# A prefix log-sum-exp scan: constants off the path to the first load, the last Exp behind the Ln of the tile above, and one late load split by partition groups

## The chip, the cores and the metric

The kernel runs on one core of a Trainium2 chip. The metric is the device time of one execution in microseconds (us), lower is better. The kernel before takes 1258.24 us (median of 4 runs, 1258.01 to 1258.38). "The trace" is one profiled execution; times in it count from the start of its span, which is about 1.8 us shorter than the device time. "Landing" means the moment at which the last of the 16 DMA engines has raised a DMA's semaphore; the trace records each of these increments.

## The reference

For each of 8 batches and 2048 columns, a running log-sum-exp over 4096 positions:

```python
out[:, 0, :] = x[:, 0, :]
for t in range(1, S):                       # S = 4096
    mx = np.maximum(out[:, t-1, :], x[:, t, :])
    out[:, t, :] = mx + np.log(np.exp(out[:, t-1, :] - mx) + np.exp(x[:, t, :] - mx))
```

Input and output are float32, 268.44 MB each.

## The kernel before

The work is cut into 64 tiles of 512 positions by 2048 columns: 128 partitions, 4 rows each, 4 MB (32 KB per partition). ScalarE (ACT) takes Exp of a quarter of a tile (512 columns), TensorE multiplies by triangular matrices of ones to get prefix sums, VectorE (DVE) adds up the 4 rows of a partition in place, ACT takes Ln, and the tile is stored. Five tile buffers go round: a load waits until the store from its buffer has landed.

```python
Li = const.tile([P, P], bf16)
masks.make_upper_triangular(nc, Li, val=1.0, diag=True)      # and Ls, Ui, Us, on POOL,
...                                                          # ahead of the block below
@block.sync
def _(sp):                                                   # the load queue
    def load(src, n):
        sp.dma_start(out=io[n][:], in_=src).then_inc(loaded[n], 16)
    for i in range(NB):                                      # NB = 5 buffers
        load(x_v[i], i)
    ...                                                      # loop over tiles 5 to 59
    for i in range(NB + turns * NB, NT):                     # tiles 60 to 63, NT = 64
        take(sp, stored[i % NB], 16)                         # wait for the store, then subtract
        load(x_v[i], i % NB)
...
@block.scalar
def _(act):                                                  # ACT, and the store queue
    def turn(n, dst_above):
        exp(n, 0)                                            # waits for loaded[n]
        if dst_above is not None:
            ln(io[(n - 1) % NB], 2)                          # last two quarters of the tile above
        exp(n, 1)
        if dst_above is not None:
            ln(io[(n - 1) % NB], 3)
            store(dst_above, (n - 1) % NB)                   # waits for 4 Ln, issues 4 MB
        exp(n, 2)
        ln(io[n], 0)
        exp(n, 3)
        ln(io[n], 1)
    ...
    # after tile 63: store its first half, then Ln and store of its last two quarters
```

The softmax here doesn't subtract the row's maximum and nothing guards it: scores larger than these inputs give would overflow.

Of the kernel before, what the change touches and what calls it, by code (L numbers as in the profile page):

```python
# [9 lines left out]
def kernel(  # L10
# [20 lines left out]
    nc = tc.nc  # L31
# [5 lines left out]
    B, S, D = x.shape  # L37
    P = 128
    R = 4
    NBLK = S // (P * R)  # L40
    NT = B * NBLK
    FD = 512
    NC = D // FD
    NB = 5
    assert NC == 4 and NBLK >= 3

    const = ctx.enter_context(tc.tile_pool(name="const", bufs=1))
    Li = const.tile([P, P], bf16)
    masks.make_upper_triangular(nc, Li, val=1.0, diag=True)
    Ls = const.tile([P, P], bf16)  # L50
    masks.make_upper_triangular(nc, Ls, val=1.0, diag=False)
    Ui = const.tile([P, P], bf16)
    masks.make_lower_triangular(nc, Ui, val=1.0, diag=True)
    Us = const.tile([P, P], bf16)
    masks.make_lower_triangular(nc, Us, val=1.0, diag=False)

    pool = ctx.enter_context(tc.tile_pool(name="io", bufs=1))
    psum = ctx.enter_context(tc.tile_pool(name="ps", bufs=1, space=bass.MemoryType.PSUM))
# [26 lines left out]
    with tc.tile_critical():  # L85
# [10 lines left out]
        chain = [sem("chain0"), sem("chain1")]  # L96
        freed = [sem("freed0"), sem("freed1")]

        with nc.Block() as block:

            @block.sync
            def _(sp):
                def load(src, n):
                    sp.dma_start(out=io[n][:], in_=src).then_inc(loaded[n], 16)

                for i in range(NB):
                    load(x_v[i], i)
                turns = (NT - NB) // NB
                with sp.Fori(0, turns) as j:
                    for n in range(NB):  # L110
                        take(sp, stored[n], 16)
                        load(x_v[bass.ds(j * NB + (NB + n), 1)][0], n)
                for i in range(NB + turns * NB, NT):
                    take(sp, stored[i % NB], 16)
                    load(x_v[i], i % NB)
                for i in range(NT - NB, NT):

                    take(sp, stored[i % NB], 48 if i == NT - 1 else 16)

            @block.scalar  # L120
            def _(act):
                def exp(n, c):
                    t = io[n]
                    if c == 0:
                        take(act, loaded[n], 16)
                    act.activation(  # L126
                        et[c][:], t[:, :, cols(c)], ACT.Exp
                    )._wait_ge(freed[c % 2], c // 2 + 1).then_inc(exps[c % 2], 1)
                    if c >= 2:
                        take(act, freed[c % 2], 2)  # L130

                def ln(t, c, told=logs):
                    act.activation(  # L133
                        t[:, :, cols(c)], t[:, :, cols(c)], ACT.Ln
                    )._wait_ge(added[c % 2], c // 2 + 1).then_inc(told, 1)
                    if c >= 2:
                        take(act, added[c % 2], 2)

                def store(dst, n):
                    take(act, logs, NC)  # L140
                    act.dma_start(out=dst, in_=io[n][:]).then_inc(stored[n], 16)

                def turn(n, dst_above):
                    exp(n, 0)
                    if dst_above is not None:
                        ln(io[(n - 1) % NB], 2)
                    exp(n, 1)
                    if dst_above is not None:
                        ln(io[(n - 1) % NB], 3)
                        store(dst_above, (n - 1) % NB)  # L150
                    exp(n, 2)
                    ln(io[n], 0)
                    exp(n, 3)
                    ln(io[n], 1)

                turn(0, None)
                turns = (NT - 1) // NB
                with act.Fori(0, turns) as j:
                    for n in range(1, NB + 1):
                        turn(n % NB, o_v[bass.ds(j * NB + (n - 1), 1)][0])  # L160
                for i in range(1 + turns * NB, NT):
                    turn(i % NB, o_v[i - 1])
                last = stored[(NT - 1) % NB]
                t = io[(NT - 1) % NB]
                take(act, logs, 2)
                act.dma_start(
                    out=o_v[NT - 1][:, :, 0:2 * FD], in_=t[:, :, 0:2 * FD]
                ).then_inc(last, 16)
                for c in range(2, NC):
                    ln(t, c, parts[c])  # L170
                    take(act, parts[c], 1)
                    act.dma_start(  # L172
                        out=o_v[NT - 1][:, :, cols(c)], in_=t[:, :, cols(c)]
                    ).then_inc(last, 16)
                take(act, freed[0], 2)
                take(act, freed[1], 2)

            @block.tensor
            def _(pe):
                def front(c, first):  # L180
                    for r in range(R):
                        m = pe.matmul(  # L182
                            ps[c][:], (Li if r == 0 else Ls)[:], et[c][:, r, :],
                            start=first and r == 0, stop=r == R - 1, skip_group_check=True,
                        )
                        if r == 0:
                            m._wait_ge(exps[c % 2], c // 2 + 1)
                    m.then_inc(prefix[c % 2], 1)
                    if c >= 2:
                        take(pe, exps[c % 2], 2)  # L190

                def total(c, final):

                    if final:
                        pe.wait_ge(copied[c % 2], [1, 2, 2, 1][c]).then_inc(freed[c % 2], 1)
                    else:
                        for r in range(R):
                            m = pe.matmul(  # L198
                                ps[c][:], (Us if r == 0 else Ui)[:], et[c][:, r, :],
                                start=False, stop=r == R - 1, skip_group_check=True,  # L200
                            )
                            if r == 0:
                                m._wait_ge(copied[c % 2], [1, 2, 2, 1][c])
                        m.then_inc(freed[c % 2], 1)
                    if c in (1, 2):
                        take(pe, copied[c % 2], 2)

                def turn(first, final):
                    for c in range(NC):
                        front(c, first)  # L210
                        total((c - 1) % NC, first if c == 0 else final)


                pe.sem_inc(freed[0], 2)
                pe.sem_inc(freed[1], 1)
                with pe.Fori(0, B):
                    turn(True, False)
                    with pe.Fori(0, NBLK - 2):
                        turn(False, False)
                    turn(False, True)  # L220
                pe.wait_ge(copied[1], 1).then_inc(freed[1], 1)
                take(pe, copied[1], 1)

            @block.vector
            def _(dve):
                def piece(t, c):
                    q, base = c % 2, 2 * (c // 2)
                    sl = cols(c)
                    dve.tensor_add(t[:, 1, sl], ps[c][:], et[c][:, 1, :])._wait_ge(  # L229
                        prefix[q], c // 2 + 1  # L230
                    ).then_inc(chain[q], 1)
                    dve.tensor_copy(t[:, 0, sl], ps[c][:]).then_inc(copied[q], 1)  # L232
                    dve.tensor_add(t[:, 2, sl], t[:, 1, sl], et[c][:, 2, :])._wait_ge(  # L233
                        chain[q], base + 1
                    ).then_inc(chain[q], 1)
                    dve.tensor_add(t[:, 3, sl], t[:, 2, sl], et[c][:, 3, :])._wait_ge(  # L236
                        chain[q], base + 2
                    ).then_inc(added[q], 1)
                    if c >= 2:
                        take(dve, prefix[q], 2)  # L240
                        take(dve, chain[q], 4)

                dve.sem_inc(copied[1], 1)
                turns = NT // NB
                with dve.Fori(0, turns):
                    for n in range(NB):
                        for c in range(NC):
                            piece(io[n], c)
                for i in range(turns * NB, NT):
                    for c in range(NC):  # L250
                        piece(io[i % NB], c)
# [30 lines left out]
```

## Time and profile before

| what | before |
|---|---|
| time | 1258.24 us |
| span of the trace | 1256.5 us |
| bytes in and out, rate over the span | 268.44 MB and 268.44 MB, 427 GB/s |
| busiest engine, ACT | 936.7 us, 75% |
| first load issued | 2.82 us |
| last landing | 1254.87 us |

These lines of the page of the kernel before are the engines' busy times, the DMA engines' busy share in tenths and the rate in GB/s over 40 equal slices, and the DMA issues (count, KB each, median us from issue to landing):

```profile
PE 605.2 (48%) x1872; PEld 196.9 (16%) x1920; DVE 659.9 (53%) x1024; ACT 936.7 (75%) x513; POOL 1.9 (0%) x12
...
DMA  8999999999999999999999999999999999999996
GB/s 377 423 433 432 433 433 433 433 432 434 432 431 432 434 434 433 434 433 434 433 434 434 434 433 432 434 434 433 432 433 433 434 431 434 432 432 431 434 434 275
...
io<-in_x_dram SPq DMA_DIRECT2D x64, 4096.0 KB, 31.5
out_dram<-io ACTq DMA_DIRECT2D x63, 4096.0 KB, 38.7
```

No compute engine is full, and the DMA engines are, at 432 to 434 GB/s in the steady part. A tile takes 19.4 us: 8.39 MB at 433 GB/s. A load needs 31.5 us from issue to landing and a store 38.7, so both queues always have work.

The timeline of ACT in the kernel before shows what that means for it. Columns: start, duration, engine, line, operation, output and input; in brackets the idle time before it and who ended it. L126 is Exp; these three are the first Exp of tiles 61, 62 and 63:

```profile
1182.72 1.91 ACT L126 ACTIVATE et<-io 128x2048 bf16<-128x2048 f32 x1 [4.31 <-ACTq L71]
...
1202.20 1.91 ACT L126 ACTIVATE et<-io 128x2048 bf16<-128x2048 f32 x1 [4.35 <-ACTq L71]
...
1221.73 1.91 ACT L126 ACTIVATE et<-io 128x2048 bf16<-128x2048 f32 x1 [4.40 <-ACTq L71]
...
1229.15 0.34 ACTq L141 DMA_DIRECT2D out_dram<-io  x1
```

The last line is the issue of tile 62's store, between tile 63's second and third Exp.

The landings say more than the busy shares. In load 61, fifteen engines are done at 1174.49 and the sixteenth at 1182.60; in load 63 at 1213.22 and 1221.61; in store 61 at 1226.52 and 1235.10. In load 0 all sixteen come within 0.62 us. One engine has fallen over 8 us behind, little by little: it is 0.24 us behind the others in load 9 and 8.39 in load 63, so some 9 ns more with each of its 32 KB pieces (an estimate, at 16 pieces per tile, 8 in and 8 out). The table by stretches of the kernel before shows the same without landings. After the time and the length of the stretch come busy times (and instruction counts) of PE, PE's weight loads, DVE, ACT and POOL, then the granted clock, the DMA share and GB/s:

```profile
1224.00:1226.00 2.00, 2.00 (x6) 0.76 (x5) 0.38 (x1) 2.00 (x2) 0.00 (x0) 0.50 0.61 262
1226.00:1228.00 2.00, 2.00 (x6) 0.44 (x4) 1.97 (x4) 2.00 (x2) 0.00 (x0) 0.50 0.08 33
1228.00:1230.00 2.00, 1.18 (x3) 0.15 (x1) 1.01 (x3) 1.50 (x2) 0.00 (x0) 0.71 0.11 49
...
1250.00:1252.00 2.00, 0.00 (x0) 0.00 (x0) 0.00 (x0) 0.00 (x0) 0.00 (x0) 0.50 0.30 111
1252.00:1254.00 2.00, 0.00 (x0) 0.00 (x0) 0.00 (x0) 0.00 (x0) 0.00 (x0) 0.50 0.07 26
```

A share of 0.07 or 0.08 is about one engine of sixteen. From 1226 to 1230 fifteen engines have nothing to do, because tile 62's store is not issued yet, and at the end they are done 4 us before the slow one.

At the other end, SP's waits in the kernel before have the wait for the last constant on POOL (total us, times, longest), and its timeline has the first loads:

```profile
SPq L85 <- POOL Us masks.py:102: 1.8, 1, 1.8
```

```profile
2.82 1.34 SPq L104 DMA_DIRECT2D io<-in_x_dram  x3
```

### The profile page before, as it was taken

Reading aid. Unit: us, or ns where it says so; the run is one execution under the profiler, and the core shown is the slowest. Engines: PE = TensorE matmul, PEld = TensorE weight load, DVE = VectorE, ACT = ScalarE, POOL = GpSimd, SP = SyncE. Lnnn points to the kernel's source line nnn. Section 1 sums busy time; section 2 is a strip of 40 time slices with the busy share of each in tenths; the row PEclk is TensorE's granted clock in tenths of the full one; section 3 lists DMA queues with packets and bytes.
Section 4 is the critical chain, followed back from the end, with each engine's and each line's share of the span. In section 5 each row is a group of like instructions: output and inputs, shape, how many; then the busy total and the mean of one; then the engine's idle time right before and its main releaser. Section 6 shows DMA issues by size and latency. Waiting matters only on the chain. (4 is left out here: it accounts for less than half of the span.)

```text
span 1256.5 us, 6996 instructions
## 1 busy us (share of the span) xinstructions
PE 605.2 (48%) x1872; PEld 196.9 (16%) x1920; DVE 659.9 (53%) x1024; ACT 936.7 (75%) x513; POOL 1.9 (0%) x12
## 2 busy tenths in 40 slices
PE   3555445454454444554445444455455444544542
PEld 1111111111111111111111111111111111111110
DVE  3656455464554544555546455464555544545443
ACT  5988778777787777877878778777787777877774
POOL 0000000000000000000000000000000000000000
PEclk9888687885888858878688786887857888578785
DMA  8999999999999999999999999999999999999996
GB/s 377 423 433 432 433 433 433 433 432 434 432 431 432 434 434 433 434 433 434 433 434 434 434 433 432 434 434 433 432 433 433 434 431 434 432 432 431 434 434 275
DMA packets 19875, 536.90 MB, mean 427 GB/s; under 512 B 2080, under 2 KB 2080, under 8 KB 3616
## 3 DMA queue, kind: packets, MB, share of 16 engines
q10 hardware_dynamic: 10656, 268.44, 49.6%
q1 hardware_dynamic: 9216, 268.44, 49.6%
q14 instruction: 3, 0.02, 0.0%
HBM read 268.44 MB, written 268.44 MB: 427 GB/s over the span
## 5 line engine op out<-in xcount | busy, mean ns | idle before, releaser
L126 ACT ACTIVATE et<-io 128x2048 bf16<-128x2048 f32 x256 | 486.5, 1901 | 302.1 <-ACTq L71 283.6
L133 ACT ACTIVATE io<-io 128x2048 f32<-128x2048 f32 x256 | 484.8, 1894 | 2.5 <-DVE io L236 1.7
L229 DVE TENSOR_TENSOR io<-ps,et 128x512 f32<-128x512 f32 x256 | 177.1, 692 | 570.9 <-PE ps L182 568.7
L182 PE MATMUL ps<-et,Li 128*128 128x512 bf16 x256 | 126.5, 494 | 628.6 <-ACT et L126 627.8
L182 PE MATMUL ps<-et,Ls 128*128 128x512 bf16 x768 | 280.9, 487 | 0.0
L198 PE MATMUL ps<-et,Ui 128*128 128x512 bf16 x624 | 213.0, 455 | 2.9 <-issue 0.4
L236 DVE TENSOR_TENSOR io<-io,et 128x512 f32<-128x512 f32 x256 | 177.1, 692 | 8.9
L233 DVE TENSOR_TENSOR io<-io,et 128x512 f32<-128x512 f32 x256 | 174.5, 681 | 0.0
L232 DVE COPY io<-ps 128x512 f32<-128x512 f32 x256 | 174.3, 681 | 0.0
L182 PEld LDWEIGHTS ps<-et,Li 128*128 128x128 bf16 x256 | 25.5, 100 | 787.4 <-ACT et L126 787.2
L182 PEld LDWEIGHTS ps<-et,Ls 128*128 128x128 bf16 x768 | 89.8, 117 | 98.1 <-issue 66.3
L198 PE MATMUL ps<-et,Us 128*128 128x512 bf16 x224 | 103.7, 463 | 0.3 <-DVE io L232 0.3
L198 PEld LDWEIGHTS ps<-et,Ui 128*128 128x128 bf16 x672 | 77.1, 115 | 113.4 <-issue 60.1
L198 PEld LDWEIGHTS ps<-et,Us 128*128 128x128 bf16 x224 | 26.1, 116 | 40.4 <-issue 22.7
L35 ACT ACT_TABLE_LOAD x1 | 1.3, 1283 | 0.8 <-PEq L266 0.8
masks.py:102 POOL TENSOR_SCALAR_AFFINE_SELECT Ui<-Ui 128x128 bf16<-128x128 bf16 x1 | 0.3, 296 | 0.0
masks.py:102 POOL TENSOR_SCALAR_AFFINE_SELECT Us<-Us 128x128 bf16<-128x128 bf16 x1 | 0.3, 295 | 0.0
masks.py:66 POOL TENSOR_SCALAR_AFFINE_SELECT Ls<-Ls 128x128 bf16<-128x128 bf16 x1 | 0.3, 294 | 0.0
masks.py:66 POOL TENSOR_SCALAR_AFFINE_SELECT Li<-Li 128x128 bf16<-128x128 bf16 x1 | 0.3, 293 | 0.0
masks.py:101 POOL MEMSET Ui<- 128x128 bf16 x1 | 0.2, 207 | 0.0
masks.py:101 POOL MEMSET Us<- 128x128 bf16 x1 | 0.2, 207 | 0.0
masks.py:65 POOL MEMSET Ls<- 128x128 bf16 x1 | 0.2, 206 | 0.0
(5 smaller groups left out, 0.6 us busy)
## 6 DMA issues: line engine op xcount, KB each, us to landing
io<-in_x_dram SPq DMA_DIRECT2D x64, 4096.0 KB, 31.5
out_dram<-io ACTq DMA_DIRECT2D x63, 4096.0 KB, 38.7
out_dram<-io ACTq DMA_DIRECT2D x1, 2048.0 KB, 11.1
out_dram<-io ACTq DMA_DIRECT2D x2, 1024.0 KB, 11.8
```

What stands on the lines that cost most here:

```text
L35: nc.scalar.preload_act_table_set("natural_log_exp_and_others")
L126: act.activation(et[c][:], t[:, :, cols(c)], ACT.Exp)._wait_ge(freed[c % 2], c // 2 + 1).then_inc(exps[c % 2], 1)
L133: act.activation(t[:, :, cols(c)], t[:, :, cols(c)], ACT.Ln)._wait_ge(added[c % 2], c // 2 + 1).then_inc(told, 1)
L182: m = pe.matmul(ps[c][:], (Li if r == 0 else Ls)[:], et[c][:, r, :], start=first and r == 0, stop=r == R - 1, skip_group_check=True,)
L198: m = pe.matmul(ps[c][:], (Us if r == 0 else Ui)[:], et[c][:, r, :], start=False, stop=r == R - 1, skip_group_check=True,)
L229: dve.tensor_add(t[:, 1, sl], ps[c][:], et[c][:, 1, :])._wait_ge(prefix[q], c // 2 + 1).then_inc(chain[q], 1)
L232: dve.tensor_copy(t[:, 0, sl], ps[c][:]).then_inc(copied[q], 1)
L233: dve.tensor_add(t[:, 2, sl], t[:, 1, sl], et[c][:, 2, :])._wait_ge(chain[q], base + 1).then_inc(chain[q], 1)
L236: dve.tensor_add(t[:, 3, sl], t[:, 2, sl], et[c][:, 3, :])._wait_ge(chain[q], base + 2).then_inc(added[q], 1)
```

## The change

It has three parts. (1) The four constants are built inside the block, and only TensorE waits for them, so that the first loads need not. (2) In the last turn, the Ln and the store of tile 62 no longer wait for load 63: its Exp comes behind them. (3) Load 61 is split: three of each partition's four rows as one DMA, the fourth row in groups of 1, 2, 3, ... 15 and 8 partitions, each group in two pieces of unequal width, 33 DMAs in all.

```diff
-    masks.make_upper_triangular(nc, Li, val=1.0, diag=True)       (and three more)
+            @block.gpsimd
+            def _(pool):                                  # the same four constants
+                for W in (Li, Ls, Ui, Us):
+                    pool.memset(W[:], 1.0).then_inc(ones, 1)
+                ... affine_select(...).then_inc(shaped, 1)
+                pe.wait_ge(shaped, 4)                     # in TensorE's stream
...
+    SPLIT = NT - 3
+    groups, lo = [], 0
+    for k in list(range(1, 16)) + [8]:
+        groups.append((lo, lo + k, 32 * len(groups) + 48))
+        lo += k
...
-                    load(x_v[i], i % NB)
+                    if i == SPLIT:
+                        t, m = io[i % NB], i % NB
+                        sp.dma_start(
+                            out=t[:, 0:R - 1, :], in_=x_v[i][:, 0:R - 1, :]
+                        ).then_inc(loaded[m], 16)
+                        for lo, hi, w in groups:
+                            for c0, c1 in ((0, w), (w, D)):
+                                sp.dma_start(
+                                    out=t[lo:hi, R - 1, c0:c1], in_=x_v[i][lo:hi, R - 1, c0:c1]
+                                ).then_inc(loaded[m], 16)
+                    else:
+                        load(x_v[i], i % NB)
...
-                def turn(n, dst_above):
-                    exp(n, 0)
+                def turn(n, dst_above, above_first=False, landings=1):
+                    if not above_first:
+                        exp(n, 0, landings)
                     if dst_above is not None:
                         ln(io[(n - 1) % NB], 2)
-                    exp(n, 1)
+                    if not above_first:
+                        exp(n, 1)
                     if dst_above is not None:
                         ln(io[(n - 1) % NB], 3)
                         store(dst_above, (n - 1) % NB)
+                    if above_first:
+                        exp(n, 0)
+                        exp(n, 1)
                     exp(n, 2)
...
-                    turn(i % NB, o_v[i - 1])
+                    turn(i % NB, o_v[i - 1], i == NT - 1, 1 + 2 * len(groups) if i == SPLIT else 1)
```

More of the change, by code (lines that the diff above doesn't have):

```diff
@@ L45 @@
     assert NC == 4 and NBLK >= 3
+    SPLIT = NT - 3
[3 more added lines that the diff above has]
+        lo += k
+    assert lo == P
     const = ctx.enter_context(tc.tile_pool(name="const", bufs=1))
     Li = const.tile([P, P], bf16)
-    masks.make_upper_triangular(nc, Li, val=1.0, diag=True)
     Ls = const.tile([P, P], bf16)
-    masks.make_upper_triangular(nc, Ls, val=1.0, diag=False)
     Ui = const.tile([P, P], bf16)
-    masks.make_lower_triangular(nc, Ui, val=1.0, diag=True)
     Us = const.tile([P, P], bf16)
-    masks.make_lower_triangular(nc, Us, val=1.0, diag=False)
     pool = ctx.enter_context(tc.tile_pool(name="io", bufs=1))
@@ L97 @@
         freed = [sem("freed0"), sem("freed1")]
+        ones, shaped = sem("ones"), sem("shaped")
         with nc.Block() as block:
+            @block.gpsimd
+            def _(pool):
+                for W in (Li, Ls, Ui, Us):
+                    pool.memset(W[:], 1.0).then_inc(ones, 1)
+                pool.wait_ge(ones, 4)
+                for W, sign, strict in ((Li, 1, 0), (Ls, 1, 1), (Ui, -1, 0), (Us, -1, 1)):
+                    pool.affine_select(
+                        out=W[:], in_=W[:], compare_op=mybir.AluOpType.is_ge, fill=0.0,
+                        base=-strict, pattern=[[sign, P]], channel_multiplier=-sign,
+                    ).then_inc(shaped, 1)
             @block.sync
@@ L121, in _, with exp @@
             def _(act):
-                def exp(n, c):
+                def exp(n, c, landings=1):
                     t = io[n]
                     if c == 0:
-                        take(act, loaded[n], 16)
+                        take(act, loaded[n], 16 * landings)
                     act.activation(
```

## The prediction

> **What bounds the kernel now.** The DMA engines. The page's slices show 9 tenths busy or more nearly throughout and 432 to 434 GB/s; ACT is at 75%, and its first Exp of a tile waits for the load (283.6 us over 95 waits, list of waits). A tile is 4 MB in and 4 MB out, about 19.4 us at that rate; 64 make some 1240 of the 1256.5 us.
>
> More exactly, one of the 16 DMA engines bounds it. The trace records each engine's increment of a DMA's semaphore. In load 0 the 16 land within 0.6 us; in load 61 fifteen by 1174.5, the last at 1182.60; in load 63 fifteen by 1213.2, the last at 1221.61; in store 61 fifteen by 1226.5, the last at 1235.10. One engine has fallen 8 to 9 us behind, by a few ns per 32 KB packet (1.21 us each). From 1221.6 to 1254.87 its landings are as close as its bytes allow (9.8 us per 4 MB DMA): it never rests, while the others idle. In the table by stretches the DMA share is 0.08 in 1226 to 1228 (one engine in sixteen), and 0.30 and 0.07 after 1250. Everything ends with the straggler's last store.
>
> **What the change does.**
> 1. Start. SP waits 1.8 us for the last mask on POOL (SP's waits) and issues its first load at 2.82. Afterwards it needs only the start barrier (0.73) and issues near 1.1. The masks are ready long before the first Exp. DMA bounds from the first byte: -1.7 us, all critical.
> 2. Last tile. Ln of tile 62's last chunks no longer waits for load 63; store 62 goes out about 6 us before its present 1229.15, which fills the fifteen engines' gap. The straggler is busy with store 61 until 1235.1 anyway: alone 0 us.
> 3. Split of tile 61's last row (1 MB). The Trainium skill, "DMA: Bandwidth & Descriptors", section on why a DMA increments its semaphore by 16, says that a DMA over k partitions (k up to 15) uses the k lowest-numbered engines. The groups then put 16 rows of 8 KB on engine 0, falling to none on engine 15, where there were 8 each. The same page ("Latency and other measured facts") calls engines 7 and 15 usually slower; the trace does not number engines, so that the straggler is 15 is my guess from the change's shape. Then it sheds 64 KB, at 1.21 us per 32 KB: -2.4 us, critical. Cost: 33 issues on SP while it would wait anyway; small packets let the low engines' stores pass, so load 61 lands a few us after 1182.6, which the buffered tiles absorb.
>
> Sum: 4.1 us; predicted **1254.2 us**, range 1252.6 to 1256.9; faster by over 2%: 0.01, within 2%: 0.98, slower: 0.01.
>
> **What shows it right.** First load issued near 1.1; store 62 issued about 8 us earlier; no DMA share near 0.1 between 1220 and 1230; the straggler's lag in load 63 reduced by 2.4 us or more; last landing near 1250.8.
>
> **What would make it wrong.** The straggler is another engine: for 7 it sheds nothing and only the start's 1.7 us or less remains (1256.6 to 1257.5), for 0 it would lose. Small reads costing far more than their bytes. Load 61 landing so late that ACT (about 14.5 us per tile) bounds the tail.

## More of the kernel before

ACT idles 4.3 to 4.4 us per tile for the load and works for the other 15.0 (8 activations at a pitch of 1.80 us, a store issue, small gaps).

## The result, and the profile after

The changed kernel takes 1260.62 us (median of 4 runs, 1260.47 to 1260.72), the kernel before 1258.24: 2.4 us slower instead of 4 us faster, and outside the predicted range. The ratio is 1.0019 (95% interval 1.0002 to 1.0036), a small loss that counts as the same time by a limit of 2%. Here and below a ratio is the mean time of one kernel's fast runs over that of the other's of the same rounds, so not quite the ratio of the medians quoted.

SP's timeline of the changed kernel shows that part 1 came as predicted; SP's list of waits has no wait for POOL any more:

```profile
1.04 2.42 SPq L120 DMA_DIRECT2D io<-in_x_dram  x5
```

The 40 slices of the changed kernel's page differ at the end: 425, 393, 386 and 304 GB/s, where there were 431, 434, 434 and 275.

```profile
DMA  9999999999999999999999999999999999999997
GB/s 400 425 431 432 434 434 432 433 434 434 433 433 433 434 433 433 433 433 433 433 434 433 432 433 433 434 433 432 433 433 433 433 432 433 433 433 425 393 386 304
```

ACT's timeline of the changed kernel (L154 is Exp, L161 Ln, L169 the store's issue) shows where the time went:

```profile
1197.81 1.91 ACT L154 ACTIVATE et<-io 128x2048 bf16<-128x2048 f32 x1 [20.89 <-ACTq L73]
...
1212.85 1.89 ACT L154 ACTIVATE et<-io 128x2048 bf16<-128x2048 f32 x1
...
1226.05 3.69 ACT L161 ACTIVATE io<-io 128x2048 f32<-128x2048 f32 x2
1230.12 1.91 ACT L161 ACTIVATE io<-io 128x2048 f32<-128x2048 f32 x1 [0.38 <-DVE io L270]
1232.13 0.34 ACTq L169 DMA_DIRECT2D out_dram<-io  x1
1232.60 5.51 ACT L154 ACTIVATE et<-io 128x2048 bf16<-128x2048 f32 x3 [0.57 <-ACTq L73]
1239.14 1.91 ACT L161 ACTIVATE io<-io 128x2048 f32<-128x2048 f32 x1 [1.03 <-DVE io L270]
```

Tile 61's first Exp starts at 1197.81 after 20.89 us of idle time; before it was 1182.72 after 4.31. Load 61 landed at 1197.71 instead of 1182.60, 15.1 us later although everything had begun 1.8 us earlier. From then on ACT never waits for a load again: tile 62's Exp begins at 1212.85 without a gap, tile 63's at 1232.60 straight after tile 62's store. The tail, which the slow DMA engine used to bound, has become a chain on ACT.

The table by stretches of the changed kernel shows its other side:

```profile
1180.00:1190.00 10.00, 0.00 (x0) 0.00 (x0) 0.00 (x0) 0.00 (x0) 0.00 (x0) 0.61 1.03 322
...
1230.00:1232.00 2.00, 0.00 (x0) 0.00 (x0) 0.09 (x1) 1.88 (x1) 0.00 (x0) 1.00 0.04 16
...
1242.00:1244.00 2.00, 1.04 (x4) 0.31 (x4) 2.00 (x4) 2.00 (x2) 0.00 (x0) 1.00 0.04 16
1244.00:1246.00 2.00, 0.00 (x0) 0.00 (x0) 1.97 (x4) 1.21 (x2) 0.00 (x0) 1.00 0.04 16
```

All compute engines stand still from 1180 to 1190, while the DMA engines are busy but move only 322 GB/s: in the record of DMA packets the small pieces took longer than their bytes (those of 6208 bytes 0.24 to 0.62 us). Twice after 1230 the DMA engines wait for ACT (shares of 0.04 in 1230 to 1232 and 1242 to 1246): the last stores are issued later (the last at 1250.09 instead of 1242.29) and the end moves from 1254.87 to 1257.43.

### The profile page after: what moved, and what is told of

Its sections match the earlier page's. It is cut to its first block, busy times and chain, and to the rows that moved or that the text cites. A ratio compares the mean times of both kernels' runs of the same rounds, so it can differ in the third digit from the quotient of the medians.

```text
span 1259.0 us, 7021 instructions
## 1 busy us (share of the span) xinstructions
PE 601.4 (48%) x1872; PEld 196.5 (16%) x1920; DVE 659.9 (52%) x1024; ACT 936.7 (74%) x513; POOL 1.9 (0%) x12
## 5 line engine op out<-in xcount | busy, mean ns | idle before, releaser
L154 ACT ACTIVATE et<-io 128x2048 bf16<-128x2048 f32 x256 | 486.2, 1901 | 308.5 <-ACTq L73 289.9
L161 ACT ACTIVATE io<-io 128x2048 f32<-128x2048 f32 x256 | 484.7, 1894 | 3.9 <-DVE io L270 3.9
## 6 DMA issues: line engine op xcount, KB each, us to landing
io<-in_x_dram SPq DMA_DIRECT2D x63, 4096.0 KB, 31.5
```

Of the source, the lines that this page charges most:

```text
L154: act.activation(et[c][:], t[:, :, cols(c)], ACT.Exp)._wait_ge(freed[c % 2], c // 2 + 1).then_inc(exps[c % 2], 1)
L161: act.activation(t[:, :, cols(c)], t[:, :, cols(c)], ACT.Ln)._wait_ge(added[c % 2], c // 2 + 1).then_inc(told, 1)
```

## The experiments

There were thirteen kernels besides the two, each in 3 or 5 rounds beside the kernel before. All gave correct results. In the table, "over" is the last landing minus that of load 61. Landings are of the one profiled execution, times are medians. The experiments were run on four chips; but in every kernel that has part 1 and splits tile 61, load 60 still lands within 0.3 us of m1_start's, so the landings that follow can be compared.

| run | time, us | before in the same rounds | ratio (95% interval) | load 61 landed | last landing | over |
|---|---|---|---|---|---|---|
| before | 1258.24 | | | 1182.60 | 1254.87 | 72.3 |
| changed kernel | 1260.62 | 1258.24 | 1.0019 (1.0002 to 1.0036) | 1197.71 | 1257.43 | 59.7 |
| m1_start | 1256.31 | 1258.26 | 0.9983 (0.9969 to 0.9997) | 1180.98 | 1253.23 | 72.3 |
| m2_start_order | 1256.83 | 1258.26 | 0.9986 (0.9973 to 1.0) | 1181.05 | 1253.32 | 72.3 |
| m3_start_split | 1260.82 | 1258.26 | 1.002 (1.0006 to 1.0034) | 1197.89 | 1257.53 | 59.6 |
| m4_row_alone | 1259.05 | 1258.26 | 1.0008 (0.9994 to 1.0021) | 1190.99 | 1255.73 | 64.7 |
| k4 | 1261.33 | 1258.62 | 1.0017 (0.9999 to 1.0034) | 1198.73 | 1258.09 | 59.4 |
| k5 | 1266.55 | 1258.62 | 1.0059 (1.0042 to 1.0076) | 1203.79 | 1263.15 | 59.4 |
| k15 | 1258.76 | 1258.62 | 1.0005 (0.9979 to 1.0031) | 1194.14 | 1254.26 | 60.1 |
| e8_row_alone | 1258.69 | 1258.31 | 1.0001 (0.9988 to 1.0014) | 1186.00 | 1255.44 | 69.4 |
| e8_split | 1271.85 | 1258.31 | 1.0108 (1.0093 to 1.0122) | 1197.73 | 1267.28 | 69.6 |
| e8_92 | 1266.45 | 1258.31 | 1.0061 (1.0041 to 1.0082) | 1193.52 | 1263.13 | 69.6 |
| stores_too | 1256.84 | 1258.31 | 0.9986 (0.9974 to 0.9999) | 1183.94 | 1253.58 | 69.6 |
| whole | 1259.60 | 1258.32 | 1.0011 (0.9997 to 1.0024) | 1197.03 | 1256.39 | 59.4 |
| relief | 1255.95 | 1258.32 | 0.9981 (0.9968 to 0.9995) | 1183.89 | 1252.86 | 69.0 |

The theory after seeing the result: part 3 is to blame, because the slow engine is not number 15, so that it got more rows instead of none, and because the added packets made load 61 late. The rivals: part 2 costs the time; a split costs nothing but the wrong engine was favoured; or packets cost DMA time by themselves.

### The parts one by one: m1_start, m2_start_order, m3_start_split

m1_start is the changed kernel without parts 2 and 3, m2_start_order without part 3, m3_start_split without part 2:

```diff
 m1_start, m2_start_order
-    SPLIT = NT - 3
+    SPLIT = -1
 m1_start, m3_start_split
-    turn(i % NB, o_v[i - 1], i == NT - 1, ...)
+    turn(i % NB, o_v[i - 1], False, ...)
```

> Part 1 alone (constants built inside the block, no split, old Exp order). All theories: 1.7 to 1.8 us faster than before (the first load is issued at 1.04 instead of 2.82 us and the slow DMA engine never rests afterwards), about 1256.5. If the time is unchanged, the start's gain is lost again somewhere and the whole account is wrong.

> Parts 1 and 2 (no split). Theory (slow DMA engine bounds the tail): within 0.3 us of m1_start, though store 62 goes out 6 us or more earlier. Rival (the Ln order bounds the tail, ACT): a gain or loss of over 1 us against m1_start.

> Parts 1 and 3 (split, old Exp order). Theory (split alone is to blame): 1259 to 1261, so over 2.5 us slower than m1_start. Rival (the new Exp order costs the time once load 61 is late and ACT is the tail's bound, as the bubbles of 0.38 and 1.03 us before Ln in the changed kernel's tail suggest): at or below 1258.5.

m1_start gained 1.95 us (medians 1256.31 and 1258.26). Part 1 is worth what the earlier issue gives (2.82 - 1.04 = 1.78).

m2_start_order shows part 2 doing exactly what it was made for, and for nothing. These are its store issue, and its table by stretches:

```profile
1219.77 0.34 ACTq L169 DMA_DIRECT2D out_dram<-io  x1
```

```profile
1220.00:1230.00 10.00, 5.85 (x16) 2.03 (x16) 5.33 (x9) 8.74 (x5) 0.00 (x0) 0.66 0.98 423
...
1246.00:1248.00 2.00, 0.00 (x0) 0.00 (x0) 0.00 (x0) 0.00 (x0) 0.00 (x0) 0.50 0.06 25
1248.00:1250.00 2.00, 0.00 (x0) 0.00 (x0) 0.00 (x0) 0.00 (x0) 0.00 (x0) 0.50 0.07 26
```

Store 62 goes out at 1219.77 (1227.51 in m1_start), the hole between 1220 and 1230 is filled (0.98), and fifteen engines are done at 1244.8 instead of 1249.3. The slow engine works on alone, at a share of 0.06 to 0.07, and lands at 1253.32 (1253.23 in m1_start). The 0.5 us between the medians is more than the 0.3 expected, but within the intervals, and the last landings differ by 0.09 us.

m3_start_split carries the whole loss: 4.5 us over m1_start, load 61 at 1197.89. It also removes the rival that part 2 harmed the changed kernel: with and without it the last landing is 1257.43 and 1257.53.

### Does any second DMA do it? m4_row_alone

```diff
-                        for lo, hi, w in groups: ...
+                        for lo, hi in [(0, P)]:           # the whole last row, 128 partitions
+                            sp.dma_start(
+                                out=t[lo:hi, R - 1, :], in_=x_v[i][lo:hi, R - 1, :]
+                            ).then_inc(loaded[m], 16)
```

> Part 1, and tile 61's last row loaded by one further DMA of 128 partitions (8 rows for each engine, as without a split). Theory (unequal rows and small packets are to blame, not a second DMA): within 0.6 us of m1_start. Rival (any second DMA for tile 61 lets the stores pass and makes load 61 late): over 1.5 us slower than m1_start.

It was the rival: 2.7 us over m1_start, although each engine carries the same bytes as before. These are its first Exp of tiles 61, 62 and 63:

```profile
1191.10 1.91 ACT L149 ACTIVATE et<-io 128x2048 bf16<-128x2048 f32 x1 [14.11 <-ACTq L69]
...
1206.96 1.91 ACT L149 ACTIVATE et<-io 128x2048 bf16<-128x2048 f32 x1 [0.74 <-ACTq L69]
...
1226.51 1.91 ACT L149 ACTIVATE et<-io 128x2048 bf16<-128x2048 f32 x1 [4.43 <-ACTq L69]
```

Load 61 landed 10.0 us after m1_start's. The trace gives the mechanism. Where both queues have work, an engine takes one piece (one packet of the trace's record) from the load queue (q1) and one from the store queue (q10) in turn, whatever their sizes. Pieces of the slow engine in the changed kernel, each starting where the one before ends (start and duration in us, queue, bytes; the record of DMA packets, followed by hand because it doesn't name engines):

```
1172.742 1.256 q10 32768
1173.995 0.920 q1  24576
1174.911 1.265 q10 32768
1176.173 0.919 q1  24576
1177.088 1.220 q10 32768
1178.304 0.009 q1      4
1178.310 1.231 q10 32768
1179.537 0.034 q1    704
```

The 4-byte piece that raises the semaphore takes a turn like any other. Each further piece in the load queue, however small, therefore lets one more 32 KB store piece (1.21 us) go ahead. m4_row_alone has 8 pieces and one of 4 bytes more per engine, so 9 turns more for the stores. A store too has 8 pieces of 32 KB and one of 4 bytes per engine, so 9 turns let 8 pieces of 32 KB pass: 8 x 1.21 = 9.7 us, measured 10.0. The packets counted over all engines agree: when load 61 landed, an engine had on average moved 471.8 store pieces of 32 KB in m1_start and 479.8 in m4_row_alone, and store 59 landed at 1198.31 instead of 1207.77.

### Which engine is slow? k4, k5 and k15

The fourth row again in two DMAs, of 124 and 4 partitions (k4), 125 and 3 (k5), 120 and 8 (k15). By the Trainium skill ("DMA: Bandwidth & Descriptors", section on why a DMA increments its semaphore by 16) a DMA takes the largest k up to 16 that divides its partitions, and the k lowest-numbered engines: 4, 5 and 15 engines here.

```diff
-                        for lo, hi in [(0, P)]:
+                        for lo, hi in [(0, 124), (124, P)]:    # k4; 125 in k5, 120 in k15
```

> Part 1, and tile 61's last row by a DMA of 124 partitions and one of 4: if a DMA uses the largest number up to 16 of engines that divides its partitions, both run on engines 0 to 3, which then carry 32 rows of 8 KB each, all others none. Theory (the slow engine is number 4): it sheds 8 rows, engines 0 to 3 become the last by a little; 0.3 to 1.5 us faster than m1_start. Rival (the slow engine is one of 0 to 3): 24 rows more on it, about 7 us slower than m1_start. Rival (it is 5 to 15): like the theory here, to be told apart by k5.

> Part 1, and tile 61's last row by a DMA of 125 partitions and one of 3: 25 rows on each of engines 0 to 4 (one more on 0 to 2), none on 5 to 15. Theory (the slow engine is number 4): 17 rows more on it at about 0.3 us, 5 us or more slower than m1_start. Rival (it is 5 to 15, 15 for one, as predicted): it sheds 8 rows, so 1 to 2.5 us faster than m1_start.

> Part 1, and tile 61's last row by a DMA of 120 partitions and one of 8: 8 rows on engines 0 to 14 (one more on 0 to 7), none on 15; only two further DMAs. This is the split's aim without its small packets. Theory (the slow engine is 4, one row more): 0 to 1.3 us slower than m1_start. Rival (it is 15 and only the small packets spoiled the split): 2 to 2.5 us faster than m1_start.

The times in these expectations were wrong, as they left out the order of the queues. The landings answer the question all the same. The first Exp of tile 61, in k4 and in k5:

```profile
1198.84 1.91 ACT L149 ACTIVATE et<-io 128x2048 bf16<-128x2048 f32 x1 [21.91 <-ACTq L69]
```

```profile
1203.90 1.91 ACT L149 ACTIVATE et<-io 128x2048 bf16<-128x2048 f32 x1 [26.87 <-ACTq L69]
```

In k5, which puts 25 rows on each of five engines, load 61 is complete but for one engine at 1192.75, and that one comes at 1203.79, 11 us later. In k4, which puts 32 rows on each of four, the last four increments lie within 1.6 us (1197.17 to 1198.73), with no straggler; the slow engine shows there in store 59, in which fifteen are done at 1197.92 and the last at 1208.59. So the slow engine is among the five and not among the four: with the skill's numbering it is engine 4. The record of pieces above agrees: the slow engine's first small piece has 704 bytes, which is the fifth group's width, so that it takes part in groups of five and more only. The split thus gave it 12 rows of 8 KB (groups of 5 to 15, and the group of 8), where it had 8. It alone ends load 61: its last piece of 6080 bytes starts at 1196.05, those of the seven other engines in the last group by 1189.72.

k15, which is the aim of the split without its small pieces, gives the slow engine 9 rows and still lands load 61 at 1194.14. It cost 2.4 us against m1_start by the medians of different chips, but its four runs spread from 1257.23 to 1263.03, so only the landing is used here.

### Is the delay absorbed early in the run? e8_row_alone, e8_split, e8_92

The same splits at tile 8 instead of tile 61, with the first turns of the loops unrolled for it; e8_92 cuts the row into 92 and 36 partitions.

```diff
-    SPLIT = NT - 3
+    SPLIT = 8
```

> As m4_row_alone, but tile 8 is split instead of tile 61 (first turns of the loops unrolled for it). Theory O (the 9 further load packets per engine each let one 32 KB store packet pass, which only hurts because tile 61 is near the end and ACT then has to catch up): the cost is absorbed, within 0.7 us of m1_start (1256.3). Rival P (a split row costs DMA time by itself): as m4_row_alone, 2 us or more over m1_start.

> As m3_start_split, but tile 8 is split instead of tile 61. Theory: what stays is what engine 4 carries in addition, 4 rows of 8 KB (1.2 us) and its 24 small packets (about 1 us): 1.2 to 2.5 us over m1_start, and below m3_start_split by 2 us or more. Rival P: as m3_start_split, 4 us over m1_start. Rival (engine 15 is the slow one): 2 us below m1_start.

> Part 1, and tile 8's last row by a DMA of 92 partitions (4 engines, 23 rows each) and one of 36 (12 engines, 3 rows each): engine 4 sheds 5 rows of 8, engines 0 to 3 carry 26 rows. Theory (engine 4 is slow, and at tile 8 the order costs nothing): 1.0 to 1.6 us faster than m1_start, about 1255. Rival (engine 4 is not the slow one, or packets cost by themselves): at or above m1_start.

All three missed, and the time of e8_row_alone is what rival P expected (2.4 us over m1_start). It is only stores_too, below, that rules rival P out. The reason of the miss is worth more than the hit would have been. The delay is not absorbed: the order that the split makes stays for the rest of the run. The DMA issues on the page of m1_start, and then of e8_row_alone (the median over all tiles, last number):

```profile
io<-in_x_dram SPq DMA_DIRECT2D x64, 4096.0 KB, 31.5
out_dram<-io ACTq DMA_DIRECT2D x63, 4096.0 KB, 38.7
```

```profile
io<-in_x_dram SPq DMA_DIRECT2D x63, 4096.0 KB, 43.6
out_dram<-io ACTq DMA_DIRECT2D x63, 4096.0 KB, 26.4
```

One split at tile 8 makes the median load 12 us slower from issue to landing and the median store 12 us faster. A load is issued when a store has landed, a store when a load has been worked on, and both queues take turns; so an advance of the stores over the loads can be handed on from tile to tile (this link is argued; no run separates it). The ninth of the sixteen engines to finish a load is 4.8 us later than in m1_start at load 10, and still at loads 20, 30 and 40. Counted to the last engine, load 10 lands 8.2 us later than in m1_start, load 60 still 4.8 and load 63 5.8 later (1225.75 against 1219.99), and the time is m4_row_alone's (1258.69 against 1259.05). The end follows load 63 by 29.7 us. In e8_split and e8_92, with more pieces on some engines, load 63 lands at 1236.61 and 1232.45, and the time grows with it (e8_92's six runs spread from 1262.30 to 1271.59, so its median is rough). That their low engines stay so far behind was not taken apart further.

### Keeping the order: stores_too

If order is the cause, cutting the stores like the load must undo it. Stores 58 and 59 get the same cut as load 61 in m4_row_alone:

```diff
-                    act.dma_start(out=dst, in_=io[n][:]).then_inc(stored[n], 16)
+                    if halves:                             # tiles 58 and 59
+                        act.dma_start(out=dst[:, 0:R - 1, :], in_=io[n][:, 0:R - 1, :]
+                        ).then_inc(stored[n], 16)
+                        act.dma_start(out=dst[:, R - 1, :], in_=io[n][:, R - 1, :]
+                        ).then_inc(stored[n], 16)
```

> As m4_row_alone, but stores 58 and 59 are cut in the same way as load 61, so that store packets no longer outnumber load packets by bytes. Theory O: load 61 lands at 1181 to 1185 instead of 1190.99, and the time returns to within 1 us of m1_start. Rival P: as m4_row_alone or slower.

It does: load 61 lands at 1183.94, and the time is 1256.84, 0.5 us from m1_start instead of 2.7. The split DMA itself costs next to nothing here; what it does to the order costs the time. Tile 61's first Exp in stores_too:

```profile
1184.05 1.91 ACT L149 ACTIVATE et<-io 128x2048 bf16<-128x2048 f32 x1 [6.71 <-ACTq L69]
```

Load 63 even lands 6.7 us earlier than in m1_start (1213.27), and the end does not move (1253.58): there the slow engine is the bound again.

### Rows or small pieces? whole

The sixteen groups of the changed kernel, each row in one piece (17 DMAs):

```diff
-                            for c0, c1 in ((0, w), (w, D)):
+                            for c0, c1 in ((0, D),):       # in effect
```

> As m3_start_split with the same sixteen groups, but each row in one piece: engine 4 keeps 12 rows, with 24 instead of 48 further load packets (its counter packets included). In m3_start_split, k4, k5 and k15 the last landing stood 59.4 to 60.1 us after load 61's. If the bytes on engine 4 set load 61's landing: within 1 us of m3_start_split's 1197.89, time about 1260.8. If the number of packets sets it: about 1193 to 1195, time 1257 to 1258.5.

Load 61 lands at 1197.03, 0.9 us before m3_start_split's: halving the number of pieces hardly helps. That fits the trace of the changed kernel, in which the slow engine's small pieces follow each other from 1192.98 on with no store piece between them: by then all stores that were waiting had gone ahead, and further pieces have none to let pass. By its landing it answers to the theory of the rows; the time, 1259.6, lies midway between the two expectations.

### Relieving the slow engine with the order kept: relief

Load 61 and store 58 both get 28 KB of each partition in one DMA and the last 4 KB in DMAs of 92 (four engines) and 36 partitions (twelve engines):

```diff
+    pieces, H = [(0, 92), (92, P)], R * D - 1024
+    sp.dma_start(out=t[:, 0:H], in_=src[:, 0:H]).then_inc(loaded[m], 16)
+    for lo, hi in pieces:
+        sp.dma_start(out=t[lo:hi, H:], in_=src[lo:hi, H:]).then_inc(loaded[m], 16)
     (and the same for store 58)
```

> Part 1, and both load 61 and store 58 cut in the same way: 28 KB of each partition in a DMA of 128 partitions, the last 4 KB in one of 92 and one of 36. Engine 4 sheds 40 KB (1.5 us) and gets as many further store packets as load packets, so the order holds. Theory: load 61 lands within 4 us of m1_start's 1180.98 and the time is 0.7 to 1.6 us below m1_start (1254.7 to 1255.6). Rival (the order on engines 0 to 3, with 26 pieces each, delays load 61 all the same): at or above m1_start.

The order held (load 61 at 1183.89), and it has the lowest median of all kernels, 1255.95 us. That is 0.36 us below m1_start's, and neither the theory (0.7 to 1.6) nor the rival (none) was met: the last landing moved by only 0.37 us against m1_start where shedding 40 KB should have given 1.5. Its ratio to the kernel before, 0.9981, can't be told from m1_start's 0.9983. What ate the rest was not looked into. Both beat the two kernels of this study, and m1_start is the simpler one.

## Why the prediction was wrong

**The bound.** Right. The kernel is bound by DMA, and its end by one slow engine. m1_start and m2_start_order behave so to within 0.5 us.

**Part 1.** Right: predicted -1.7, measured -1.95 by medians and -1.6 by the last landing, with the first load at 1.04 as predicted.

**Part 2.** Right: predicted an earlier store 62, a filled hole and no gain by itself; all three in m2_start_order.

**Part 3.** Wrong, in two steps.

The first is "that the straggler is 15 is my guess from the change's shape. Then it sheds 64 KB". It is engine 4, shown by k4 against k5 and by the 704-byte piece. It carries 32 KB more instead of 64 KB less: +1.2 us (an estimate, at 1.21 us per 32 KB) where -2.4 was entered. The prediction named this risk, but only for engines 7 and 0. The row of the skill's page that names 7 and 15 also calls its supposed cause specific to DMAs that software describes; these are issued from SP and ACT, and the trace calls their queues hardware_dynamic. The guess was thus weaker than the prediction made it.

The second would have gone unpunished only with much more slack: "load 61 lands a few us after 1182.6, which the buffered tiles absorb". It landed 16.7 us after m1_start's 1180.98. Of that, 10.0 us come with a second DMA alone, of equal rows (m4_row_alone). The rest comes with the groups: nearly all of it is there without the small pieces (whole, 16.1 us). And there is little to absorb it. Once load 61 is in, ACT needs 59.4 to 60.1 us to the last landing when it never waits for a load again, as in six kernels (changed kernel, m3_start_split, k4, k5, whole, and k15 but for 0.36 us), whose loads landed up to 9.7 us apart. In m1_start the same stretch is 72.3 us. The slack is 72.3 - 59.5 = 12.8 us, and the loss is the delay beyond it. The 59.5 comes from the same runs, so the table tests only that one figure fits them all:

| kernel | load 61 after m1_start's | less 12.8 | last landing after m1_start's, measured |
|---|---|---|---|
| changed kernel | 16.7 | 3.9 | 4.2 |
| whole | 16.1 | 3.3 | 3.2 |
| k4 | 17.8 | 5.0 | 4.9 |
| k5 | 22.8 | 10.0 | 9.9 |

The start's gain moved the last landing from 1254.87 to m1_start's 1253.23, by 1.6 us; 4.2 - 1.6 = 2.6 us, and the kernel became 2.4 us slower. m4_row_alone doesn't fit this one rule: its load 61 is within the slack, but its load 63 came 6.4 us late (1226.40), and from there its end follows in 29.3 us (29.7 in e8_row_alone). Both are the same thing, a late load in front of a chain on ACT. "Load 61 landing so late that ACT bounds the tail" stands in the prediction among what could make it wrong; it was given too little weight, because the prediction counted the bytes of the two queues and not their turns.

What stays open: why engine 4 needs a little longer per piece (its store pieces took 1.22 to 1.27 us in the stretch shown, 1.213 on most others), and what the split would have done had the slow engine been 15; by that numbering no DMA on these queues leaves out engine 4 alone.

## What to carry to other kernels

When two DMA queues are both full, as here, their order is a resource: they took turns by pieces, so cutting a transfer on one queue handed bandwidth to the other, and in this loop of loads and stores the shift stayed to the end; cut both alike or neither. Before giving one DMA engine less work, find out which engine is slow, with two DMAs that differ in one engine (124 and 125 partitions), rather than from its usual number. And before delaying anything near the end, measure the slack from that point to the last landing: here 12.8 us, which looked like the cover of five buffers and was less than one tile.

## What the Trainium skill lacked or had wrong

- "DMA: Bandwidth & Descriptors", section "Latency and other measured facts", calls engines 7 and 15 usually slower, and its supposed cause specific to software-described DMAs. The DMAs here are of the other kind, so this is a case beside that row more than against it. Here the slow one is engine 4: with five engines one straggles by 11 us (k5), with four none does (k4). It fell 8.4 us behind by load 63 in the kernel before.
- The same page, section "Queues, rings and completion order", says that an engine drains a whole packet, typically 9 to 17 descriptors, from one ring before it switches. In the records followed here it switched after every single piece of 24 or 32 KB, and the 4-byte semaphore piece took a turn too. This contradicts the page if such a piece is one descriptor; the count fits that (9 pieces per engine and tile in each queue, 8 of data and one of 4 bytes), but the trace doesn't say it.
- The page states that an engine goes round its queues, but not what follows for a kernel, that cutting a transfer on one queue lets the other queue pass: 10.0 us later for load 61 with one further DMA (m4_row_alone), and a median load of 43.6 us from issue to landing instead of 31.5 (e8_row_alone).
- The same page's choice of engines (largest k up to 16 that divides the partitions) is borne out: the 124-, 125- and 120-partition rows raised the semaphore from 4, 5 and 15 engines. Which numbers these engines have, no trace here says.
